# Out projection and the whole second MLP product as seven products; operand tiles moved by 32 bytes

## Chip, core and metric

One core of one Trainium2 chip runs the kernel in one launch. The metric is the device time of the launch in microseconds. TensorE does the matmuls, VectorE and ScalarE prepare their operands and read their results, GpSimd computes a few columns, SyncE and GpSimd issue DMAs.

## Reference

The kernel computes one layer of a streaming encoder on x of 512 frames by 1024 channels, all in float32:

```
h    = rmsnorm(x);  zu, zv, zq, zf, zi, zo, g_a, g_b = split(h @ w_in)
y_a  = gmlp_branch(zu, zv) @ w_up_a
y_b  = hgrn2_branch(zq, zf, zi, zo) @ w_up_b
mix  = sigmoid(g_a) * y_a + sigmoid(g_b) * y_b
x    = x + mix @ w_out                       # 1024 x 1024
h    = rmsnorm(x)
x    = x + square(relu(h @ w_ff1)) @ w_ff2   # 1024 x 4096, 4096 x 1024
out  = rmsnorm(x)
```

## The kernel before

**Products.** A float32 product is made of three matmuls of reduced-precision parts: `split` writes a high part H (ScalarE, a copy with rounding) and a low part L (VectorE, source minus H), and `mm3` multiplies H by H, H by L and L by H. `operand` splits a weight tile of 128 x 1024 into the rings `WH` and `WL` of five buffers each; `wload` loads it first by DMA on SyncE's queue into the ring `raw` of four buffers. So every weight tile costs one long ScalarE row and one long VectorE row.

**Seven products.** A product of 2 x 2 blocks can be made from seven products of sums of blocks in place of eight. Before the change this is so for the two merge gates and for ff1 (`seven`, 256-wide matmuls, partial sums on ScalarE and VectorE), and for channel tiles c=1, 2, 3 (of 1024 of the 4096 channels each) of the second MLP product, ff2. There the tile's activations `act` of 1024 channels by 512 frames fall into four quarters a[i,j] (i: half of the frames, j: half of the channels) and its weights into b11, b12, b21, b22. The weight sums w1 = b12 + b11 and w3 = b22 + b12 are made by a second DMA that adds to the tile (on GpSimd's queue, `accum_op`), the further sums w1 + b22 and w4 + w1 by VectorE, which also makes the sums of the activations (E, and in place) and the low parts `aL`, `WL`; ScalarE makes the high parts `aH`, `WH`. Each of the seven products is 24 matmuls, 512 wide, into two PSUM banks: X (tag `hm`), Z (`acc`), Y5 (`y`), Y3.

**Plain products.** The upb product (w_up_b), the out projection (w_out) and the first tile of ff2 (c=0, its eight tiles f < `NSLOW`) are plain. For the out projection the loop over channels d splits `mix` into mixH and mixL (192 matmuls, in two halves `hf` of the output columns and four frame tiles t); after each frame tile of the second half `norm_to_T` makes the norm: squares on ScalarE, the root on GpSimd, the scaled rows `xn` on VectorE, four transposes `pt` on TensorE, and the split of those into h2H and h2L. ff1 begins with four plain tiles (`NPLAIN`) in two halves of the frames; the first half needs h2 of frame tiles t=0 and 1.

**Order and memory.** A scheduler sets the order of the instructions on each engine when the program is built; on the chip each engine takes them in that order and waits at semaphores. The pool `po2` (E, aH, aL with three buffers, `rawx` for weights with six) lies where h2 and its sums lay, so nothing may be loaded there before ff1's last product has ended. The pool `pmix` holds mix.

Of the kernel before, what the change touches and what calls it, by code (L numbers as in the profile page):

```python
# [79 lines left out]


# [100 lines left out]


# [696 lines left out]
```

## Time and profile before

| what | us |
|---|---|
| time, median of 3 (lowest to highest) | 850.44 (847.4 to 851.98) |
| the profiled execution: its own time | 850.19 |
| its span in the profile | 848.4 |
| TensorE busy | 831.3 |
| VectorE busy | 637.3 |
| ScalarE busy | 401.4 |

The span is the time from the first to the last recorded instruction of that one execution; its own time is 1.8 us longer. Its mean granted TensorE clock is 0.995 of full speed. A matmul's recorded duration overlaps the next one's, so what a matmul costs is read from the distance of two starts.

### The profile page before, as it was taken

What the parts mean: (1) busy time and instruction counts of PE and PEld (TensorE: products, weight loads), DVE (VectorE), ACT (ScalarE), POOL (GpSimd) and SP (SyncE); (2) the same over time, 40 slices, a digit from 0 to 9 for tenths busy, and PEclk for the clock granted to TensorE, in tenths of its full rate; (3) what the DMA queues carried; (4) which work ended last, traced back from release to release, by engine and by line L of the source; (5) the groups of instructions that cost most, each with busy time, mean ns of one, the idle gap of its engine ahead of it and who ended that gap; (6) DMA issues with size and microseconds to landing.
All of it is one profiled execution on the core that took longest, in us unless ns stands there. A gap on an engine that the chain in (4) does not pass through costs nothing.

```text
span 848.4 us, 13369 instructions
## 1 busy us (share of the span) xinstructions
PE 831.3 (98%) x5282; PEld 748.2 (88%) x5282; DVE 637.3 (75%) x1092; ACT 401.4 (47%) x644; POOL 47.6 (6%) x79
## 2 busy tenths in 40 slices
PE   8999999999999999999999999899999999999996
PEld 6989898989889997999988889899999988777884
DVE  6563888979799587788565349877777574899996
ACT  6433434333342335556533333777766642545464
POOL 2000000000001000000000012000000000010103
PEclk9999999999999999999999999999999999999998
DMA  9233212121221122133423412222322285194812
GB/s 330 88 121 110 100 51 75 51 75 51 75 75 50 51 76 75 54 121 106 147 100 122 162 62 100 70 105 101 120 105 101 100 290 182 28 280 101 233 27 99
DMA packets 26912, 92.68 MB, mean 109 GB/s; under 512 B 3361, under 2 KB 3873, under 8 KB 26850
## 3 DMA queue, kind: packets, MB, share of 16 engines
q1 hardware_dynamic: 24546, 84.49, 28.1%
q0 software_dynamic: 1728, 6.29, 4.0%
q10 hardware_dynamic: 576, 1.05, 0.3%
q8 instruction: 41, 0.67, 0.3%
q14 instruction: 21, 0.17, 0.1%
HBM read 89.72 MB, written 2.10 MB: 108 GB/s over the span
## 4 chain that ended last, share of the span: by engine, by line
PE 88%; DMA 4%; DVE 3%; issue 2%; ACT 2%; POOL 0%; SPq 0%; POOLq 0%; ACTq 0%; DVEq 0%
PE acc L114 14%; PE acc L113 14%; PE acc L115 14%; PE prodx L115 5%; PE prodx L113 5%; PE prodx L114 5%; DMA raw<-in_w_dram 4%; PE prodzy L115 4%; PE prodzy L114 4%; PE prodzy L113 4%; PE sp L437 4%; PE hm L115 2%; PE hm L114 2%; PE hm L113 2%; PE y L113 2%
## 5 line engine op out<-in xcount | busy, mean ns | idle before, releaser
L90 DVE TENSOR_TENSOR WL<-raw,WH 128x1024 fp32r<-128x1024 f32 (+1 forms) x134 | 152.0, 1137 | 102.5 <-ACT WH L89 102.0
L89 ACT ACTIVATE WH<-raw 128x1024 fp32r<-128x1024 f32 (+1 forms) x134 | 132.4, 989 | 184.7 <-PE acc L114 68.4
L113 PE MATMUL acc<-WH,hTH 128*128 128x256 f32 x320 | 91.7, 287 | 0.5 <-ACT hTH L89 0.5
L115 PE MATMUL acc<-WH,hTL 128*128 128x256 f32 x320 | 91.6, 286 | 0.0
L114 PE MATMUL acc<-WL,hTH 128*128 128x256 f32 x320 | 90.6, 283 | 0.0
L115 PE MATMUL acc<-hTH,WL 128*128 128x512 f32 x160 | 64.3, 402 | 0.0
L114 PE MATMUL acc<-hTL,WH 128*128 128x512 f32 x160 | 64.1, 401 | 0.0
L113 PE MATMUL acc<-hTH,WH 128*128 128x512 f32 x160 | 64.1, 400 | 0.0
L90 DVE TENSOR_TENSOR WL<-s,WH 128x1024 fp32r<-128x1024 f32 x44 | 53.8, 1222 | 10.5 <-ACT WH L89 9.6
L113 PEld LDWEIGHTS acc<-WH,hTH 128*128 128x128 f32 x320 | 60.4, 189 | 0.7 <-ACT hTH L89 0.7
L115 PEld LDWEIGHTS acc<-WH,hTL 128*128 128x128 f32 x320 | 60.4, 189 | 0.1
L114 PEld LDWEIGHTS acc<-WL,hTH 128*128 128x128 f32 x320 | 60.3, 189 | 0.0
L89 ACT ACTIVATE WH<-s 128x1024 fp32r<-128x1024 f32 x44 | 46.7, 1061 | 14.1 <-PE prodx L114 8.7
L446 DVE COPY_PREDICATED scores<-mask,sp 128x192 f32<-128x192 int32 (+2 forms) x144 | 43.9, 358 | 6.8 <-PE sp L437 6.4
L114 PE MATMUL hm<-WL,aH 128*128 128x512 f32 x96 | 38.1, 397 | 0.0
L115 PE MATMUL hm<-WH,aL 128*128 128x512 f32 x96 | 38.0, 396 | 0.0
L113 PE MATMUL hm<-WH,aH 128*128 128x512 f32 x96 | 37.9, 396 | 0.0
L437 PE MATMUL sp<-QX,K 128*128 128x192 f32 x192 | 35.9, 326 | 0.0
L115 PEld LDWEIGHTS acc<-hTH,WL 128*128 128x128 f32 x160 | 30.1, 188 | 6.4
L114 PEld LDWEIGHTS acc<-hTL,WH 128*128 128x128 f32 x160 | 30.1, 188 | 6.4
L113 PEld LDWEIGHTS acc<-hTH,WH 128*128 128x128 f32 x160 | 30.1, 188 | 6.2
L89 ACT ACTIVATE WH<-rawx 128x1024 fp32r<-128x1024 f32 x24 | 25.1, 1052 | 19.3 <-issue 10.7
(298 smaller groups left out, 2417.1 us busy)
## 6 DMA issues: line engine op xcount, KB each, us to landing
raw<-in_w_dram SPq DMA_DIRECT2D x128, 512.0 KB, 3.5
rawx<-in_w_dram SPq DMA_DIRECT2D x18, 512.0 KB, 8.5
rawx<-in_w_dram POOLq DMA_DIRECT2D x6, 512.0 KB, 6.4
raw<-in_w_dram POOLq DMA_DIRECT2D x6, 512.0 KB, 9.0
x_t<-in_x_dram SPq DMA_DIRECT2D x4, 512.0 KB, 6.1
x<-in_x_dram SPq DMA_DIRECT2D x4, 512.0 KB, 5.7
out_dram<-x ACTq DMA_DIRECT2D x4, 256.0 KB, 2.8
out_dram<-x SPq DMA_DIRECT2D x4, 256.0 KB, 2.4
```

The costliest lines, as they stand in the source:

```text
L89: nc.scalar.activation(H, src, AF.Copy)
L90: nc.vector.tensor_tensor(L, src, H.bitcast(F32), ALU.subtract)
L113: nc.tensor.matmul(acc, ah, bh, start=first and i == 0, stop=False, **kw)
L114: nc.tensor.matmul(acc, ah, bl, start=False, stop=False, **kw)
L115: nc.tensor.matmul(acc, al, bh, start=False, stop=last and i == n - 1, **kw)
L437: nc.tensor.matmul(sp[:, j * 192:(j + 1) * 192].rearrange("p (g c) -> p g c", g=g), K[:, t * P:(t + 1) * P], QX[:, t * g:(t + 1) * g, 1:7, ...
L446: nc.vector.copy_predicated(scv[:, :, i0:i0 + n, :], mv[:, :, x0:x0 + n, :], spv[:, :, x0:x0 + n, :])
```

## The change

A class `Eighth` holds the seven products of one tile. It is used for the out projection (operand: quarters of mix, no longer split in the loop over d; `aH`, `aL` with two buffers; sums w1, w3 in `rawx` of `pmix`) and for all four channel tiles of ff2. 24 matmuls fewer are issued in each of the two places, 1624 of width 512 in place of 1672. For the out projection and for c=0 the products come as p1 (a11 b11), p2 (a12 w4), p5 (E w1), and then p6, and so on; w1 of c=0 is in `rawx`, no longer in `raw`. The norm of frame tiles 2 and 3 moves into the first stage of ff1, that of 0 and 1 stands around p4. `shift(pool)` puts a tile of 32 bytes into four pools, so that what is placed behind it in the pool moves by 32 bytes.

```diff
+    def shift(pool):
+        pool.tile([P, 8], F32, name="shift")
...
+    class Eighth:
+        def __init__(self, a, kind, c, pool, near=("b11", "w1"), bufs=3):
+            self.a, self.pool, self.bufs = a, pool, bufs
+            def fresh(name, *parts):
+                ts = [wp.tile([P, 1024], F32, tag="raw", bufs=4, name=name) if name in near else
+                      pool.tile([P, 1024], F32, tag="rawx", bufs=6, name=name) for k in range(2)]
+                for k, t in enumerate(ts):
+                    nc.sync.dma_start(t, A["w"][index[(kind, c, *parts[0], k)]])
+                    if len(parts) > 1:
+                        nc.gpsimd.dma_start(t, A["w"][index[(kind, c, *parts[1], k)]], accum_op=ALU.add)
+                setattr(self, name, ts)
+            parts = {"b11": [(0, 0)], "w1": [(0, 1), (0, 0)], "b22": [(1, 1)], "w4": [(1, 0)],
+                     "w3": [(1, 1), (0, 1)]}
+            for name in (*near, *(n for n in parts if n not in near)):
+                fresh(name, *parts[name])
+        def add(self, x, y):
+            for k in range(2):
+                nc.vector.tensor_tensor(x[k], x[k], y[k], ALU.add)
+        def operands(self, src, ring=False):
+            if ring:
+                return tuple(p.rearrange("p (k t) -> p k t", k=4) for p in operand(src, True))
+            H = self.pool.tile([P, 4, 256], F32R, tag="aH", bufs=self.bufs, name="aH")
+            L = self.pool.tile([P, 4, 256], F32R, tag="aL", bufs=self.bufs, name="aL")
+            split(src, H, L)
+            return H, L
+        def product(self, acc, hl, w, first, last, between=None):
+            H, L = hl
+            W = [operand(w[k]) for k in range(2)]
+            for i in range(2):
+                mm3(acc[i], [((H[:, k, i * P:(i + 1) * P], L[:, k, i * P:(i + 1) * P]),
+                              blk(W[k // 2], k % 2, 512)) for k in range(4)], (first, last))
+                if between and not i:
+                    between()
+        def p1(self, X, ring=False):
+            self.product(X, self.operands(self.a[0, 0], ring), self.b11, True, False)
+        def p2(self, Z, first, last):
+            self.product(Z, self.operands(self.a[0, 1]), self.w4, first, last)
+        def p5(self, Y5, first, last):
+            a = self.a
+            e = self.pool.tile([P, 4, 256], F32, tag="E", bufs=1, name="E")
+            nc.vector.tensor_tensor(e, a[1, 1], a[1, 0], ALU.subtract)
+            self.product(Y5, self.operands(e), self.w1, first, last)
+            nc.vector.tensor_tensor(a[1, 0], a[0, 0], a[1, 0], ALU.subtract)
+            nc.vector.scalar_tensor_tensor(a[0, 0], e, -1.0, a[0, 0], ALU.mult, ALU.subtract)
+            self.add(self.w1, self.b22)
+        def p6(self, X):
+            self.product(X, self.operands(self.a[0, 0]), self.w1, False, False)
+        def p7(self, X):
+            self.product(X, self.operands(self.a[1, 0]), self.w3, False, False)
+        def p3(self, Y3, first, last):
+            a = self.a
+            nc.vector.scalar_tensor_tensor(a[0, 1], a[0, 1], -1.0, a[0, 0], ALU.mult, ALU.subtract)
+            self.product(Y3, self.operands(a[0, 1]), self.b22, first, last)
+        def p4(self, X, between=None):
+            self.add(self.w4, self.w1)
+            self.product(X, self.operands(self.a[1, 1]), self.w4, False, True, between)
...
+    shift(pya)
...
+    shift(pt)
...
-    mixH = pmix.tile([P, KD, S], F32R, name="mixH")
-    mixL = pmix.tile([P, KD, S], F32R, name="mixL")
+    mix = pmix.tile([P, KD, S], F32, name="mix")
+    quarters = {(i, j): mix[:, 4 * j:4 * j + 4, 256 * i:256 * i + 256] for i in range(2) for j in range(2)}
...
-        nc.vector.tensor_tensor(sb, part[0][:, d, :], sb, ALU.add)
-        split(sb, mixH[:, d, :], mixL[:, d, :])
+        nc.vector.tensor_tensor(mix[:, d, :], part[0][:, d, :], sb, ALU.add)
+    proj = Eighth(quarters, "w_out", 0, pmix, ("b11", "w4"), 2)
...
+    shift(pr3)
...
-    for hf in range(2):
-        W = [wload("out", hf, k) for k in range(4)]
-        cs = slice(hf * 512, (hf + 1) * 512)
-        for t in range(NT):
-            acc = ps.tile([P, S], F32, tag="acc", bufs=2, name="acc")
-            tt = slice(t * P, (t + 1) * P)
-            mm3(acc, [((mixH[:, k, tt], mixL[:, k, tt]), blk(W[k // 2], k % 2, 512)) for k in range(KD)])
-            nc.vector.tensor_tensor(x2[:, t, cs], x2[:, t, cs], acc, ALU.add)
+    def add_to(l, m, src):
+        for i in range(2):
+            c = x2[:, 2 * l + i, m * S:(m + 1) * S]
+            nc.vector.tensor_tensor(c, c, src[i], ALU.subtract if m else ALU.add)
+    def squares2(l, m):
+        for i in range(2):
+            t = 2 * l + i
             junk = pn.tile([P, S], F32, tag="junk", bufs=1, name="junk")
-            mean_square(junk, x2[:, t, cs], ssq2[:, t, hf:hf + 1])
-            if hf == 1:
-                norm_to_T(pn, x2[:, t, :], t, ssq2[:, t, :], [gbc2[:, :S], gbc2[:, S:]], h2H, h2L)
+            mean_square(junk, x2[:, t, m * S:(m + 1) * S], ssq2[:, t, m:m + 1])
+    def norm2(t):
+        norm_to_T(pn, x2[:, t, :], t, ssq2[:, t, :], [gbc2[:, :S], gbc2[:, S:]], h2H, h2L)
+    def pair(name):
+        b = ps_f.tile([P, 2, S], F32, tag="zy", bufs=2, name=name)
+        return b[:, 0, :], b[:, 1, :]
+    X = [ps.tile([P, S], F32, tag="acc", bufs=2, name=f"X{i}") for i in range(2)]
+    proj.p1(X)
+    add_to(0, 0, X)
+    Y = pair("Z")
+    proj.p2(Y, True, True)
+    add_to(0, 0, Y)
+    squares2(0, 0)
+    Y = pair("Y5")
+    proj.p5(Y, True, True)
+    shift(pmix)
+    add_to(0, 1, Y)
+    add_to(1, 1, Y)
+    proj.p6(X)
+    add_to(0, 1, X)
+    Y = pair("Y3")
+    proj.p3(Y, True, True)
+    add_to(0, 1, Y)
+    squares2(0, 1)
+    proj.p7(X)
+    add_to(1, 1, X)
+    squares2(1, 1)
+    norm2(0)
+    proj.p4(X, lambda: norm2(1))
+    add_to(1, 0, X)
+    squares2(1, 0)
...
+            if half == 0 and f in (1, 2):
+                norm2(f + 1)
+    pn_stack.close()
...
-    for f in range(NSLOW):
-        aT[f] = operand(act[f])
-        W2[f] = wload("ff2", f)
-        if f < NSLOW - 2:
-            for t in range(NT):
-                for hf in range(2):
-                    ff2(f, t, hf)
-    for t in range(NT):
-        for hf in range(2):
-            for f in range(NSLOW - 2, NSLOW):
-                ff2(f, t, hf)
-            c = x2[:, t, hf * S:(hf + 1) * S]
-            nc.vector.tensor_tensor(c, c, eight[2 * t + hf], ALU.add)
...
+    for c in range(NF // 8):
+        one, end = c == 0, c == NF // 8 - 1
         a = {(i, j): acts[c][:, 4 * j:4 * j + 4, 256 * i:256 * i + 256] for i in range(2) for j in range(2)}
...
+        e = Eighth(a, "w_ff2", c, po2, ("b11", "w4") if one else ("b11", "w1"))
+        e.p1(X, one)
         add_to(0, 0, X)
+        if one:
+            e.p2(Z, True, False)
+        e.p5(Y5, one, end)
         if end:
             add_to(0, 1, Y5)
             add_to(1, 1, Y5)
+        e.p6(X)
         add_to(0, 1, X)
+        if not one:
+            e.p2(Z, False, end)
         if end:
             add_to(0, 0, Z)
             squares(0, 0)
             scaled(0, 0)
+        e.p7(X)
         add_to(1, 1, X)
         if end:
             squares(1, 1)
             scaled(1, 1)
+        e.p3(Y3, one, end)
         if end:
             add_to(0, 1, Y3)
             squares(0, 1)
             finish(0, 0)
+        e.p4(X)
```

What `shift` does to the addresses is read from the allocation of the two built programs. For each matmul, the addresses of the moving operand and of the weights are compared modulo 64 bytes: they are at equal places or 32 bytes apart. Matmuls by group:

| group (width) | before | after |
|---|---|---|
| in-projection on hT (512): 480 | apart | apart |
| upa on ya (512): 96 | apart | equal |
| 16 others of the gMLP branch (512) | equal | equal |
| upb on yb (512): 192 | equal | equal |
| out projection (512): 192, after 168 | apart | equal |
| ff2 c=0 (512): 192, after 168 | equal | equal |
| ff2 c=1 to 3 (512): 504 | apart | equal |
| on hT, and sums beside h2 and hT that lie apart (256): 1848 | apart | apart |
| t1, t2, t4 of the gates: 288, on h2: 864 (256) | equal | apart |

The first place where the order matters is VectorE at the end of the out projection and the start of ff1. Before, it reads (x_4794 is the residual rows, raw_5193 to raw_5205 weights of ff1):

```order
L619 TENSOR_TENSOR x_4794<-x_4794,acc 128x512
L228 SCALAR_TENSOR_TENSOR xn<-x_4794,rr_n,g_ffn 128x512 x2
L619 TENSOR_TENSOR x_4794<-x_4794,acc 128x512
L228 SCALAR_TENSOR_TENSOR xn<-x_4794,rr_n,g_ffn 128x512 x2
L90 TENSOR_TENSOR h2L<-pt,h2H 128x4x128 x2
L619 TENSOR_TENSOR x_4794<-x_4794,acc 128x512
L228 SCALAR_TENSOR_TENSOR xn<-x_4794,rr_n,g_ffn 128x512 x2
L90 TENSOR_TENSOR WL<-raw_5193,WH 128x1024
L90 TENSOR_TENSOR WL<-raw_5199,WH 128x1024
L90 TENSOR_TENSOR h2L<-pt,h2H 128x4x128 x2
L90 TENSOR_TENSOR WL<-raw_5205,WH 128x1024
L619 TENSOR_TENSOR x_4794<-x_4794,acc 128x512
```

After, the rows at that place are these (X_4823 and X_4824 are the two banks of X; raw_5475 and raw_5477 are the first weights of ff1's seven products, s their sums; the xn of t=0 and 1 are ahead of them):

```order
L702 TENSOR_TENSOR x_4803<-x_4803,X_4824 128x512
L92 TENSOR_TENSOR WL<-raw_5189,WH 128x1024
L702 TENSOR_TENSOR x_4803<-x_4803,X_4823 128x512
L92 TENSOR_TENSOR h2L<-pt,h2H 128x4x128 x2
L143 TENSOR_TENSOR s_5479<-raw_5477 128x512
L150 TENSOR_TENSOR s_5480<-raw_5475,raw_5477 128x512
L92 TENSOR_TENSOR WL<-raw_5195,WH 128x1024
L702 TENSOR_TENSOR x_4803<-x_4803,X_4824 128x512
L144 TENSOR_TENSOR s_5479<-s_5479,raw_5475 128x512
L92 TENSOR_TENSOR WL<-raw_5475,WH 128x1024
L310 SCALAR_TENSOR_TENSOR xn<-x_4803,rr_n,g_ffn 128x512 x2
L92 TENSOR_TENSOR h2L<-pt,h2H 128x4x128 x2
```

The first pair of h2L is that of frame tile 0 and the last pair that of frame tile 1; the read of the last X (X_4824 for the second time, the end of p4), a sum, a weight split and xn of frame tile 2 stand ahead of it. Before, the last read of the out projection (the last row of L619) stands behind the h2L of tile 1. From the row of L674 that reads the last upb product to the first of the last pair, the stretch has 29 rows of 1024 elements, 24 of 512 and 6 xn.

The second place is VectorE in ff2's first tile, c=0, of the changed program (act_5173 is the tile's activations, act_5174 those of c=1, w_7221 and w_7222 the two halves of w4, w_7225 and w_7226 those of w1, b_7231 the first of b22, hm the banks of X):

```order
L92 TENSOR_TENSOR WL<-w_7222,WH 128x1024
L246 TENSOR_TENSOR act_5173<-act_5173 128x4x256
L92 TENSOR_TENSOR aL<-act_5173,aH 128x1024
L247 SCALAR_TENSOR_TENSOR act_5173<-E,act_5173 128x4x256
L92 TENSOR_TENSOR aL<-E,aH 128x1024
L702 TENSOR_TENSOR x_4803<-x_4803,hm_7209 128x512
L258 SCALAR_TENSOR_TENSOR act_5173<-act_5173 128x4x256
L92 TENSOR_TENSOR aL<-act_5173,aH 128x1024
L244 TENSOR_TENSOR E<-act_5174 128x1024
L92 TENSOR_TENSOR aL<-act_5173,aH 128x1024
L246 TENSOR_TENSOR act_5174<-act_5174 128x4x256
L92 TENSOR_TENSOR WL<-w_7225,WH 128x1024
```

On ScalarE the same place reads:

```order
L91 ACTIVATE WH<-w_7222 128x1024
L162 ACTIVATE act_5176<-prodx 128x256
L91 ACTIVATE aH<-act_5173 128x1024
L772 ACTIVATE act_5176<-act_5176 128x1024
L91 ACTIVATE aH<-E 128x1024
L91 ACTIVATE aH<-act_5173 128x1024 x2
L91 ACTIVATE WH<-w_7225 128x1024
L91 ACTIVATE WH<-w_7226 128x1024
```

The low and high parts of all four operands and the start of c=1's E stand ahead of w1's split on VectorE; on ScalarE the operand of p7 stands ahead of it. Before, the eight plain tiles had one `WL` of activations and one of weights each there.

## Rows read from the trace of the kernel before

**Rows 1.** The page: busy us (share of span) and instructions of the engines.

```profile
PE 831.3 (98%) x5282; PEld 748.2 (88%) x5282; DVE 637.3 (75%) x1092; ACT 401.4 (47%) x644; POOL 47.6 (6%) x79
```

**Rows 2.** Windows in ff2: busy us (count) of PE, PEld, DVE, ACT, POOL; clock; DMA.

```profile
733.00:773.00 40.00, 39.10 (x165) 30.82 (x166) 38.63 (x39) 21.09 (x22) 3.49 (x4) 1.00 0.66 184
773.00:812.00 39.00, 39.00 (x169) 31.41 (x168) 36.94 (x38) 21.51 (x22) 3.50 (x4) 1.00 0.59 162
```

**Rows 3.** Timeline of PE: start, duration, line, form; upb and out projection.

```profile
457.55 0.39 PE L113 MATMUL acc<-ybH,WH 128*128 128x512 f32 x1
...
463.00 0.39 PE L113 MATMUL acc<-WH,mixH 128*128 128x512 f32 x1
...
468.59 0.40 PE L113 MATMUL acc<-WH,mixH 128*128 128x512 f32 x1
```

**Rows 4.** Timeline of PE: the 256-wide matmuls of the in-projection and ff1.

```profile
28.32 0.28 PE L113 MATMUL acc<-WH,hTH 128*128 128x256 f32 x1
...
31.88 0.28 PE L113 MATMUL acc<-WH,hTH 128*128 128x256 f32 x1
...
513.72 0.28 PE L113 MATMUL acc<-h2H,WH 128*128 128x256 f32 x1
...
520.91 0.28 PE L113 MATMUL acc<-h2H,WH 128*128 128x256 f32 x1
```

**Rows 5.** Timeline of VectorE: rows back to back, and the last upb read.

```profile
463.20 0.69 DVE L590 TENSOR_TENSOR part<-acc,part 128x512 f32<-128x512 f32 x1 [2.29 <-PE acc L115]
...
505.82 1.41 DVE L228 SCALAR_TENSOR_TENSOR xn<-x,rr_n,g_ffn 128x512 f32<-128x512 f32 x2 [1.88 <-POOL rr_n L209]
507.16 2.35 DVE L90 TENSOR_TENSOR WL<-raw,WH 128x1024 fp32r<-128x1024 f32 x2
509.43 1.28 DVE L90 TENSOR_TENSOR h2L<-pt,h2H 128x512 fp32r<-128x512 f32 x2
510.63 1.22 DVE L90 TENSOR_TENSOR WL<-raw,WH 128x1024 fp32r<-128x1024 f32 x1
```

**Rows 6.** The page: a group of splits on ScalarE; busy us, mean ns.

```profile
L89 ACT ACTIVATE WH<-rawx 128x1024 fp32r<-128x1024 f32 x24 | 25.1, 1052 | 19.3 <-issue 10.7
```

**Rows 7.** Timeline of PE: start of ff1.

```profile
510.17 0.66 PE L232 MATMUL pt<-ident,xn 128*128 128x128 f32 x4 [0.26 <-DVE h2L L90]
510.58 0.37 PE L114 MATMUL acc<-h2L,WH 128*128 128x256 f32 x1
```

**Rows 8.** Timeline of PE: first matmul of ff2, and the last of all.

```profile
676.07 0.40 PE L113 MATMUL hm<-WH 128*128 128x512 f32 x1
...
840.30 0.40 PE L115 MATMUL hm<-WH,aL 128*128 128x512 f32 x1
```

**Rows 9.** The page: DMA issues, KB each, median us to landing.

```profile
rawx<-in_w_dram SPq DMA_DIRECT2D x18, 512.0 KB, 8.5
rawx<-in_w_dram POOLq DMA_DIRECT2D x6, 512.0 KB, 6.4
raw<-in_w_dram POOLq DMA_DIRECT2D x6, 512.0 KB, 9.0
```

**Rows 10.** Timeline of PE: start of the gates' seven products.

```profile
335.29 0.38 PE L113 MATMUL prodx<-hTH,WH 128*128 128x256 f32 x1 [0.96 <-ACT WH L89]
...
336.56 0.39 PE L115 MATMUL prodx<-hTH,WL 128*128 128x256 f32 x1 [0.76 <-DVE WL L90]
...
337.72 0.38 PE L115 MATMUL prodx<-hTH,WL 128*128 128x256 f32 x1
...
341.14 0.30 PE L113 MATMUL prodx<-t2H,WH 128*128 128x256 f32 x1
```

**Rows 11.** Windows there and after the end of PE's work; clock as above.

```profile
338.00:339.00 1.00, 1.00 (x6) 1.00 (x6) 1.00 (x2) 1.00 (x3) 0.00 (x0) 0.50 0.93 369
844.00:846.00 2.00, 0.00 (x0) 0.00 (x0) 0.64 (x1) 0.61 (x1) 0.00 (x0) 0.50 0.80 299
```

More of the change, by code (lines that the diff above doesn't have):

```diff
@@ L29 @@
 NF = DFF // P
-NSLOW = 8
 RADIX = [1, 4, 16]
@@ L61, in _plan @@
     names += [("upb", d) for d in range(8)]
-    for hf in range(2):
-        names += [("out", hf, k) for k in range(4)]
+    names += [("w_out", 0, j, l, k) for j, l in QUARTERS for k in range(2)]
     names += [("ff1", f) for f in range(NF)]
-    names += [("ff2", f) for f in range(NSLOW)]
-    for c in range(NSLOW // 8, NF // 8):
-        names += [("ff2q", c, j, l, k) for j, l in QUARTERS for k in range(2)]
+    for c in range(NF // 8):
+        names += [("w_ff2", c, j, l, k) for j, l in QUARTERS for k in range(2)]
     return names
@@ L90, in split, with operand @@
         nc.vector.tensor_tensor(L, src, H.bitcast(F32), ALU.subtract)
-    def operand(src):
-        n = src.shape[-1]
+    def operand(src, quarter=False):
+        n = 1024 if quarter else src.shape[-1]
         H = wp.tile([P, 1024], F32R, tag="WH", bufs=NOPER, name="WH")
         L = wp.tile([P, 1024], F32R, tag="WL", bufs=NOPER, name="WL")
-        split(src, H[:, :n], L[:, :n])
+        if quarter:
+            split(src, *(p.rearrange("p (k t) -> p k t", k=4) for p in (H, L)))
+        else:
+            split(src, H[:, :n], L[:, :n])
         return H, L
@@ L689, in trunk_kernel @@
     X, Z, Y5, Y3 = banks(ps, "hm"), banks(ps, "acc"), banks(ps2, "y5"), banks(ps2, "y3")
-    ms = po2.tile([P, NT, 2], F32, name="ms")
-    def add_to(l, m, src):
-        for i in range(2):
-            c = x2[:, 2 * l + i, m * S:(m + 1) * S]
-            nc.vector.tensor_tensor(c, c, src[i], ALU.subtract if m else ALU.add)
+    ms = po2.tile([P, NT, 4], F32, name="ms")
     def squares(l, m):
@@ L719, in finish @@
             nc.scalar.dma_start(out[t * P:(t + 1) * P, m * S:(m + 1) * S], early)
[L721 to L757 removed]
+    for c in range(NF // 8):
+        one, end = c == 0, c == NF // 8 - 1
+        a = {(i, j): acts[c][:, 4 * j:4 * j + 4, 256 * i:256 * i + 256] for i in range(2) for j in range(2)}
+        e = Eighth(a, "w_ff2", c, po2, ("b11", "w4") if one else ("b11", "w1"))
+        e.p1(X, one)
         add_to(0, 0, X)
[L759 to L761 removed]
+        if one:
+            e.p2(Z, True, False)
+        e.p5(Y5, one, end)
         if end:
@@ L764, in trunk_kernel @@
             add_to(1, 1, Y5)
-        nc.vector.tensor_tensor(a[1, 0], a[0, 0], a[1, 0], ALU.subtract)
-        nc.vector.scalar_tensor_tensor(a[0, 0], e, -1.0, a[0, 0], ALU.mult, ALU.subtract)
-        add(w1, b22)
-        product(X, a[0, 0], w1, False, False)
+        e.p6(X)
         add_to(0, 1, X)
-        product(Z, a[0, 1], w4, one, end)
+        if not one:
+            e.p2(Z, False, end)
         if end:
@@ L774, in trunk_kernel @@
             scaled(0, 0)
-        add(w4, w1)
-        product(X, a[1, 0], w3, False, False)
+        e.p7(X)
         add_to(1, 1, X)
@@ L780, in trunk_kernel @@
             scaled(1, 1)
-        nc.vector.scalar_tensor_tensor(a[0, 1], a[0, 1], -1.0, a[0, 0], ALU.mult, ALU.subtract)
-        product(Y3, a[0, 1], b22, one, end)
+        e.p3(Y3, one, end)
         if end:
@@ L786, in trunk_kernel @@
             finish(0, 0)
-        product(X, a[1, 1], w4, False, True)
+        e.p4(X)
         add_to(1, 0, X)
@@ L819, in _weight_tiles @@
             t = chan(i["w_up_b"][0], name[1] * P, KD)
[L820 to L821 removed]
         elif kind == "ff1":
             t = chan(i["w_ff1"][0], name[1] * P, KD)
[L824 removed]
+        else:
             _, c, j, l, k = name
[L826 to L828 removed]
+            t = tok(i[kind][0], (8 * c + 4 * j + 2 * k) * P, 2, l * 512, 512)
         tiles.append(t)
```

45 lines of the change are left out of this document (removed).

## Prediction, made before the result was seen

> **What bounds the kernel now.** First the page's busy shares: TensorE is busy for 98% of the span and VectorE for 75% [rows 1], so a matmul less is worth its own time wherever nothing else becomes late. Then the windows of the second MLP product, which already runs as seven products for its channel tiles 1 to 3: in each stretch of 39 to 40 us VectorE is busy for 37 to 38.6 us beside TensorE's 39 [rows 2]. There the two engines are level, and that is the form of work that the change spreads. The reader is to see this first: seven products cost TensorE an eighth less, and VectorE far more (sums of weight and operand tiles, and splits of the sums).
>
> **Prices.** Starts in the timelines of the engines.
> - A 512-wide matmul: 24 of the upb product take 463.00 - 457.55 = 5.45 us, 227 ns each; the 24 of the out projection behind them take 5.59, 233 ns each [rows 3]. By the addresses (table in the section on the change) the operands of the first lie at equal places modulo 64 bytes, those of the second 32 bytes apart.
> - A 256-wide matmul: 60 of ff1's first stage in 7.19 us, 119.8 ns (equal places); 30 of the in-projection in 3.56, 118.7 ns (32 apart) [rows 4]. So the sign is the other way round, and the change moves each width to its better side. That the address is the cause is my reading; these rows also differ in their tiles.
> - VectorE, back to back: two 1024-wide rows 2.27 us, 1.135 each; two 512-wide 1.20, 0.60 each; two xn 1.34, 0.67 each [rows 5].
> - A split on ScalarE, 1024 wide: 1.05 us [rows 6].
>
> **A rule against the shift.** The Trainium skill, "TensorE: Matmul & The Clock Gate", Part 2, "Step-by-step: what each phase is for", says that TensorE reads its moving operand and its weights through two independent SBUF ports. By that the 32 bytes would change nothing; the 227 and 233 ns of [rows 3] do not bear it out as far as they go, and it stands below as a rival.
>
> **Out projection.** It loses 24 matmuls and the other 168 get the better place: 192 x 0.233 = 44.7 us become 168 x 0.227 = 38.1, which by TensorE alone is -6.6. But what has to be ready for ff1 comes from VectorE. Count from the end of the last upb product (463.20, where VectorE starts to read it [rows 5]). In the order of the changed program, from that row to the h2L of t=1, on which the third matmul of ff1 waits, VectorE has 29 rows 1024 wide, 24 of 512 and 6 of xn: 29 x 1.135 + 24 x 0.60 + 6 x 0.67 = 51.3 us without any idle time. TensorE has already met waits by then, the longest at p3: the split of its operand is the 19th long row, with ten short ones ahead, 27.6 us, where TensorE is at about 24.5. It would reach the matmul on h2L at about 46. Before, it was there at 510.58 - 463.20 = 47.4, with one group of four transposes more behind it (0.4) [rows 7]. So the stage ends 51.3 + 0.4 - 47.4 = **+4.3** later in place of 6.6 earlier. The order itself shows why: the read of the last X and xn of t=2 stand ahead of the h2L of t=1. Even if VectorE had kept up, after the last product of p4 there come 2 x 0.60 + 1.135 + 1.34 + 0.60 = 4.3 us of VectorE rows, so that the h2L could not come before 38.1 + 0.8 (the eight transposes of t=0) + 4.3 = 43.2: 43.2 + 0.4 - 47.4 = -3.8 is the other bound, and I take the sum of the rows, which has no idle time in it.
>
> **Second product, c=0.** 24 matmuls go. Count from the first matmul on it at 676.07 [rows 8]; twelve 256-wide matmuls of ff1 follow it in both programs (1.4 us). By TensorE alone the tile is 168 x 0.227 + 1.4 = 39.5 us. The weight w1 = (0,1)+(0,0) of this tile is new and lies where h2 lay, so its load starts when ff1 has ended, about 0.8 us in (behind g_fin); with 8.5 us for a load and 6.4 for the sum by DMA it lands at 15.7, or with the longer 9.0 at 18.3 [rows 9], and that would move the next number by 2 us at most. VectorE starts on E when the twelve narrow matmuls are done, 12 x 0.227 + 1.4 = 4.1, and from there to the split of w1's first half, it included, has 12 long rows and a short one: 4.1 + 12 x 1.135 + 0.60 = 18.3. By ScalarE alone: it splits a10 into a buffer that Z's operand has until 48 x 0.227 + 1.4 = 12.3, which takes until 13.4 [rows 6], and w1 only behind it; VectorE then has three long rows, 16.8, and no earlier w1 could change that. TensorE gets to the third matmul of Y5, which needs this split, at 50 x 0.227 + 1.4 = 12.8. Wait: 5.5. Next late is b22: its split stands eleven long rows behind, 18.3 + 12.5 = 30.8, where TensorE is at 18.3 + 48 x 0.227 = 29.2. Wait: 1.6. So c=0 ends at 39.5 + 5.5 + 1.6 = 46.6.
>
> **Second product, c=1 to 3.** The form is the old one with 227 for 233 ns: 3 x 38.1 = 114.4. VectorE's 29 long and 8 short rows of such a tile take 37.7, so there is hardly slack; I leave about the idle time that one window shows, 1.0 for the three (40.0 - 39.1 [rows 2]). The tail stays: 848.4 - 840.30 = 8.1 from the start of the last matmul [rows 8]. Together 46.6 + 114.4 + 1.0 + 7.9 (the last 0.2 of the tail's matmul is counted already) = 169.9, where before has 848.4 - 676.07 = 172.3: **-2.4**.
>
> **The rest.** The 96 matmuls on ya gain 6 ns each, 0.6; the 1152 narrow ones that move gain 1.1 ns, 1.3: **-1.9**. Norm of t=2, 3 inside ff1's first stage, the longer `ms` and the moved splits of mix lie beside matmuls: VectorE is already past more of its rows there than before, since the wait has let it catch up.
>
> **The clock.** Two waits of 1 us, ended at 335.29 and 336.56, were followed by a granted clock of 0.50 (the 1.2 GHz level), the next 16 matmuls taking 341.14 - 337.72 = 3.4 us, 214 ns each in place of 119: 1.5 us lost. At the end, idle from 840.7, it is at 0.50 in 844 to 846, as it was in 338 to 339 [rows 10, 11]. The changed program has three new waits of 3.1, about 5 and 5.5 us. I take the loss of one such fall, **+1.5** (bounds: none, and three times 3.4/2 = 1.7).
>
> **Sum.** +4.3 - 2.4 - 1.9 + 1.5 = +1.5 on the profiled execution's 850.19, which lies 0.25 below the median: **about 852**.
>
> **Rivals.**
> - *VectorE does not hold it up* (shorter rows on other addresses, or fewer waits than counted; the 37 us of 39 that it managed with TensorE at full pace speak for it, the row sum against): -3.8 in the out stage, c=0 with the least wait of 4.0 (16.8 - 12.8), 43.5 and so -5.5 in ff2, -1.9, no clock loss: 839; with no wait at all it would be 850.2 - 6.6 - 10.5 - 1.9 = 831. Faster, 0.20.
> - *The clock falls at every new wait* (p3, start of ff1, Y5): 3 x 1.7 = 5.1 for 1.5: 855.3. It decides from the third fall on. Slower, 0.12. The fall at 338 speaks for it; that there one fall answers to two waits speaks against.
> - *VectorE bounds c=1 to 3 as well*: each takes the 40.0 of the window at 733 again, not 38.5: +4.5, 856.2. It decides once VectorE's rows take over 39.5 us per tile in place of 37.7. Slower, 0.09.
> - *The 32 bytes do nothing*: c=1 to 3 get 1.0 longer each (less the 1.0 of waits that go), c=0 0.5, the rest 1.9: +4.4, 856. Slower, 0.09. By the rule of the Trainium skill it would be this one.
>
> **How the numbers follow.** My forecast has 0.47 and by itself 848 to 856; 0.03 stays for what I have not thought of. Half a per cent, what a measurement of this kernel tells from no change, is 846.2 to 854.7. Faster: the first rival and a little, 0.21. Same: 0.39 of the forecast and 0.04 of the others, 0.43. Slower: the rest, 0.36. The range reaches into the first rival, 843, and over the last three, 859.
>
> **What would show it.** Right: a wait of 4 to 6 us of the matmul acc on h2L for VectorE at the start of ff1, with no idle VectorE ahead of it; one of 4 to 6 us at the first Y5 for w1's split; 227 ns spacings in ya, the out stage and ff2, and 38.2 us per tile in c=1 to 3. Wrong: out stage under 47 us, no wait at Y5, spacings of 233, or a clock of 0.50 in long stretches.

## The result and the profile after

The changed kernel takes 863.43 us (median of 4 runs, 862.53 to 865.13) where the kernel before takes 849.02 (4 runs, 847.4 to 851.98): a ratio of 1.0167, interval 1.0139 to 1.0195. It is slower by 14.4 us, outside the range that was given. The execution profiled here took 863.53, its span is 861.8.

The page's busy line of the changed kernel, which answers to [rows 1]:

```profile
PE 827.1 (96%) x5234; PEld 742.6 (86%) x5234; DVE 679.4 (79%) x1126; ACT 417.7 (48%) x654; POOL 56.7 (7%) x87
```

TensorE does 48 matmuls fewer and is busy for 4.2 us less in a span that is 13.4 us longer: 17.6 us of new idle time. And 48 matmuls less should have taken 11 us from its busy time (48 x 0.23), not 4.2: some of those that remain run slower. The list of TensorE's waits from the end of upb on (us in total, times, longest) says for whom:

```profile
PE y L118 <- ACT WH L91: 8.2, 2, 4.2
PE acc L119 <- DVE h2L L92: 4.2, 1, 4.2
PE Y L120 <- DVE aL L92: 3.4, 2, 2.9
PE hm L118 <- ACT act L162: 1.3, 1, 1.3
```

And the timeline of TensorE says where (start, duration, line, form, idle time ahead of it; the pairs of rows without a wait serve to read a spacing, below):

```profile
464.04 0.39 PE L118 MATMUL X<-WH,aH 128*128 128x512 f32 x1
...
471.52 0.39 PE L118 MATMUL Z<-WH,aH 128*128 128x512 f32 x1
...
489.35 0.50 PE L120 MATMUL Y<-WH,aL 128*128 128x512 f32 x1 [2.90 <-DVE aL L92]
...
515.55 0.58 PE L119 MATMUL acc<-h2L,WH 128*128 128x256 f32 x1 [4.16 <-DVE h2L L92]
...
679.32 0.40 PE L118 MATMUL hm<-WH 128*128 128x512 f32 x1
...
684.97 0.50 PE L118 MATMUL hm<-WH 128*128 128x512 f32 x1 [1.30 <-ACT act L162]
...
697.56 0.73 PE L118 MATMUL y<-WH,aH 128*128 128x512 f32 x2 [3.97 <-ACT WH L91]
...
727.78 0.40 PE L120 MATMUL hm<-WH,aL 128*128 128x512 f32 x1
732.37 0.75 PE L118 MATMUL y<-WH,aH 128*128 128x512 f32 x2 [4.19 <-ACT WH L91]
...
769.64 0.39 PE L118 MATMUL hm<-WH,aH 128*128 128x512 f32 x1
...
774.54 0.40 PE L118 MATMUL hm<-WH,aH 128*128 128x512 f32 x1
...
775.24 0.63 PE L118 MATMUL y<-WH,aH 128*128 128x512 f32 x2
...
814.44 0.63 PE L118 MATMUL y<-WH,aH 128*128 128x512 f32 x2
```

With the first read of the last upb product (461.52, first row of the next block) these give the stages, each against the same two rows of before ([rows 5], [rows 7], [rows 8]):

| stretch | before | after | difference | forecast |
|---|---|---|---|---|
| start to the last upb read | 463.2 | 461.5 | -1.7 | -0.9, without the clock |
| to the first matmul on h2L | 47.4 | 54.0 | +6.6 | +3.9 |
| to the first matmul of ff2 | 165.5 | 163.8 | -1.7 | -0.6, without the clock |
| to the end of the span | 172.3 | 182.5 | +10.2 | -2.4 |

(The +4.3 of the out stage was made of this +3.9 and 0.4 for transposes that move behind the mark, here in the third row.) The forecast's sign was right in three stretches, but in the first and the third that is partly luck. In the first, the first matmul on ya starts 1.4 us later in this execution (309.99 for 308.56), and the clock's fall of before at 338 does not occur. In the third, the clock costs 2.5 us (below), and a wait that before has in ff1 is not there any more (list of TensorE's waits of before):

```profile
PE prodx L113 <- ACT WH L89: 1.6, 1, 1.6
```

Most of the miss is in ff2.

**Out stage.** The timeline of VectorE, the changed kernel:

```profile
461.52 0.69 DVE L674 TENSOR_TENSOR part<-acc,part 128x512 f32<-128x512 f32 x1 [2.89 <-PE acc L120]
...
496.02 1.23 DVE L92 TENSOR_TENSOR WL<-w,WH 128x1024 fp32r<-128x1024 f32 x1 [2.12 <-ACT WH L91]
...
501.47 2.76 DVE L310 SCALAR_TENSOR_TENSOR xn<-x,rr_n,g_ffn 128x512 f32<-128x512 f32 x4 [0.17 <-POOL rr_n L291]
...
513.48 1.41 DVE L310 SCALAR_TENSOR_TENSOR xn<-x,rr_n,g_ffn 128x512 f32<-128x512 f32 x2
514.81 0.68 DVE L92 TENSOR_TENSOR h2L<-pt,h2H 128x512 fp32r<-128x512 f32 x1
```

And that of ScalarE, with two rows of ff2 for the next point:

```profile
494.92 1.06 ACT L91 ACTIVATE WH<-w 128x1024 fp32r<-128x1024 f32 x1 [7.90 <-PE Y L120]
...
696.45 1.06 ACT L91 ACTIVATE WH<-w 128x1024 fp32r<-128x1024 f32 x1 [1.94 <-DMA w<-in_w_dram]
...
731.26 1.06 ACT L91 ACTIVATE WH<-w 128x1024 fp32r<-128x1024 f32 x1 [7.82 <-DMA w<-in_w_dram]
```

From the last upb read at 461.52 to the h2L of t=1 at 514.81 VectorE takes 53.3 us. The prediction's 51.3 us of rows include that h2L row; the rows ahead of it are 50.7 of them. Idle time of 2.12 us at 496.02 and of 0.17 at 501.47 makes 2.3 us of the difference; the other 0.3 is rows a little longer than counted. The reader follows that wait across three engines: VectorE waits for ScalarE's high part, ScalarE has waited until 494.92 for TensorE to release a buffer of the ring with product Y, and TensorE is late there because of its own 2.90 us at 489.35, which was for VectorE, and of the half clock behind that (below). A wait on one engine came back to it through the ring of operands.

**ff2.** The two long waits, at 697.56 and 732.37, are both for ScalarE's split of w1, and both times the bracket of that split in the block above names the load. The wait in c=0 was forecast. The one in c=1 was not; the queues of c=1's w1 show why. SyncE's loads:

```profile
708.14 9.47 SPq L202 DMA_DIRECT2D w<-in_w_dram  x6
```

GpSimd's adding loads:

```profile
721.15 0.86 POOL L204 DMA_DIRECT2D w<-in_w_dram  x1 [2.22 <-DMA w<-in_w_dram]
726.52 0.86 POOL L204 DMA_DIRECT2D w<-in_w_dram  x1 [4.51 <-DMA w<-in_w_dram]
```

In c=0 it is w4 that lies in the ring `raw` beside b11, and p4, the last product, still reads it. w1 of c=1 wants that ring, so its load is among the last of the row that ends at 708.14 + 9.47 = 717.6, the second adding load is issued at 726.52, and ScalarE can split only at 731.26. Before, w1 stood in `raw` in each of the tiles in seven products (c=1 to 3) and its buffers came free in the middle of the tile. From the starts in the block of TensorE, c=0 took 48.7 us (679.32 to the end of its last product, 727.78 + 0.23), c=1 47.2 (to 775.24) and c=2 39.2 (to 814.44), where 46.6 and three times 38.1, with 1.0 of idle time for the three, were forecast.

**The clock.** Windows of the changed kernel (busy us and count of PE, PEld, DVE, ACT, POOL; granted clock; DMA):

```profile
488.00:492.00 4.00, 2.65 (x9) 2.15 (x10) 4.00 (x6) 0.00 (x0) 0.00 (x0) 0.83 0.00 0
492.00:496.00 4.00, 4.00 (x15) 3.17 (x14) 1.89 (x2) 1.06 (x1) 0.00 (x0) 0.75 0.25 77
...
516.00:520.00 4.00, 4.00 (x21) 4.00 (x21) 4.00 (x6) 0.60 (x1) 0.00 (x0) 0.50 0.38 131
...
700.00:704.00 4.00, 4.00 (x15) 3.17 (x14) 4.00 (x5) 1.06 (x1) 0.00 (x0) 0.72 0.64 126
...
736.00:740.00 4.00, 4.00 (x11) 3.10 (x10) 4.00 (x5) 1.61 (x2) 0.00 (x0) 0.53 0.00 0
740.00:780.00 40.00, 40.00 (x173) 32.25 (x172) 37.87 (x38) 21.54 (x21) 3.45 (x4) 1.00 0.62 178
```

Behind each of the four waits of 2.9 us and more the granted clock falls to or towards 0.50, the 1.2 GHz level. From the starts of the matmuls in these stretches, against their spacing at full clock, the falls cost 1.6 us in the out stage, 2.5 at the start of ff1 and 3.8 in ff2 (1.3 and 2.5). The fall of before at 338 [rows 11] does not occur in this execution. ff2's +10.2 is then, to 0.1: waits +10.5 (12.3 for 1.8, with the slower starts of the matmuls right behind them), clock +3.8, matmuls -4.4 (672 of 233.3 ns for 192 of 227 and 504 of 233.3), and 0.2 at the end.

### The profile page after: what moved, and what is told of

The parts are those of the page before. It is cut to its first block, busy times and chain, and to the rows that moved or that the text cites. A ratio compares the mean times of both kernels' runs of the same rounds, so it can differ in the third digit from the quotient of the medians.

```text
span 861.8 us, 13356 instructions
## 1 busy us (share of the span) xinstructions
PE 827.1 (96%) x5234; PEld 742.6 (86%) x5234; DVE 679.4 (79%) x1126; ACT 417.7 (48%) x654; POOL 56.7 (7%) x87
## 4 chain that ended last, share of the span: by engine, by line
PE 84%; DVE 7%; DMA 4%; ACT 2%; issue 2%; POOL 0%; SPq 0%; POOLq 0%; ACTq 0%; DVEq 0%
PE acc L119 13%; PE acc L120 13%; PE acc L118 12%; PE prodx L120 5%; PE prodx L118 5%; PE prodx L119 5%; DMA w<-in_w_dram 4%; PE sp L520 4%; PE prodzy L119 4%; PE prodzy L120 4%; PE prodzy L118 4%; DVE WL L92 3%; PE hm L118 3%; PE hm L119 3%; PE hm L120 3%
## 5 line engine op out<-in xcount | busy, mean ns | idle before, releaser
L92 DVE TENSOR_TENSOR WL<-raw,WH 128x1024 fp32r<-128x1024 f32 x100 | 110.9, 1109 | 74.1 <-ACT WH L91 73.5
L91 ACT ACTIVATE WH<-raw 128x1024 fp32r<-128x1024 f32 x100 | 96.4, 966 | 123.8 <-PE acc L119 50.4
L91 ACT ACTIVATE WH<-w 128x1024 fp32r<-128x1024 f32 x50 | 52.3, 1055 | 78.6 <-DVE w L216 13.8
L92 DVE TENSOR_TENSOR WL<-w,WH 128x1024 fp32r<-128x1024 f32 x50 | 60.8, 1224 | 12.6 <-ACT WH L91 12.6
L119 PE MATMUL hm<-WL,aH 128*128 128x512 f32 x120 | 47.7, 398 | 0.0
L120 PE MATMUL hm<-WH,aL 128*128 128x512 f32 x120 | 47.7, 397 | 0.0
L118 PE MATMUL hm<-WH,aH 128*128 128x512 f32 x120 | 47.6, 399 | 0.0
L204 POOL DMA_DIRECT2D w<-in_w_dram x20 | 17.6, 878 | 415.7 <-DMA w<-in_w_dram 254.3
```

The costliest lines, as they stand in the source:

```text
L91: nc.scalar.activation(H, src, AF.Copy)
L92: nc.vector.tensor_tensor(L, src, H.bitcast(F32), ALU.subtract)
L118: nc.tensor.matmul(acc, ah, bh, start=first and i == 0, stop=False, **kw)
L119: nc.tensor.matmul(acc, ah, bl, start=False, stop=False, **kw)
L120: nc.tensor.matmul(acc, al, bh, start=False, stop=last and i == n - 1, **kw)
L204: nc.gpsimd.dma_start(t, A["w"][index[(kind, c, *parts[1], k)]], accum_op=ALU.add)
```

## The experiments

Each is compared with runs of the kernel before on the same chip; a ratio has its 95% interval behind it. Diffs are against the changed kernel where nothing else is said.

### Where the time went: one part back at a time

**Out projection plain again**, ff2 as changed (the loop over `hf` and t of before):

```diff
-    proj = Eighth(quarters, "w_out", 0, pmix, ("b11", "w4"), 2)
...
+    for hf in range(2):
+        W = [wload("out", hf, k) for k in range(4)]
```

> The changed kernel with the plain out projection of before; all four tiles of ff2 in seven products and the shifts stay. Theory: the stage from upb to ff1 goes back to 47.4 us and no clock falls behind it, 8 to 10 us off, 854 to 856. Rival (the loss is all in ff2): 862 or more.

Measured: 856.91 us, ratio 1.0105 (1.0085 to 1.0124). The waits of TensorE from 460 us on keep the two on w1:

```profile
PE y L119 <- ACT WH L92: 7.3, 2, 3.8
```

**c=0 plain again**, out projection as changed:

```diff
+    for f in range(NSLOW):
+        aT[f] = operand(act[f])
+        W2[f] = wload("ff2", f)
...
-    for c in range(NF // 8):
+    for c in range(1, NF // 8):
```

> The changed kernel with tile c=0 of ff2 as eight plain tiles, as before; out projection in seven products and the shifts stay. Theory: ff2 is as before (170.9 us from ff1's end, measured so there), so the stage from the last upb product to ff1 and the clock behind it is what is left: 6.65 + about 2.5 of the clock, less 2 to 4 that the shifts give: 852 to 856. Rival (the out projection costs nothing, all of the loss is in ff2): 846 or less.

Measured: 852.69 us, 1.005 (1.0032 to 1.0068). Behind the start of ff1 no wait over 0.7 us is left, that of c=1 is gone as well: it was a consequence of what c=0 does.

**The shifts alone**, in the kernel before (diff against it):

```diff
+    shift(pya)
...
+    shift(pt)
...
+    shift(pr3)
...
-    ms = po2.tile([P, NT, 2], F32, name="ms")
+    ms = po2.tile([P, NT, 4], F32, name="ms")
```

> The kernel before with nothing but the moved addresses of the change (32 bytes in the pools of ya, of the gates' sums and of h2, and the longer ms). Theory (the address sets the spacing of the matmuls): the 1152 narrow ones on h2 and on the gates' sums go from 119.7 to about 116.8 ns (3.3 us), the 96 on ya from 233 to 228 (0.5 us), aH of ff2 stays at 233: 3 to 4 us faster than before. Rival (operand and weights have ports of their own, the address is nothing): no change, and the spacings of the changed kernel had another cause.

Measured: 845.17 us, 0.9943 (0.9928 to 0.9959), 4.2 us faster. The narrow matmuls on h2, in equal places before, are now 32 bytes apart; 15 of them (timeline of TensorE, first and sixteenth) take 1.75 us, 116.7 ns each, for 119.8 in [rows 4]:

```profile
516.51 0.28 PE L117 MATMUL acc<-h2H,WH 128*128 128x256 f32 x1
...
518.26 0.28 PE L117 MATMUL acc<-h2H,WH 128*128 128x256 f32 x1
```

The traces say the same by stages. The out stage takes 47.4 us with the plain out projection and 54.0 with the plain c=0; from the first matmul of ff2 to the end it is 181.7 and 172.3, where before has 47.4 and 172.3.

So the three parts by themselves: the shifts -4.2; the seven products of the out projection 4.7 + 4.2 = +8.9 (from c=0 plain, which has the shifts); those of c=0 8.9 + 4.2 = +13.1. Their sum, 17.8, is 3.4 more than the 14.4 measured. In the profiled executions both partial kernels show the clock's fall at 338 and the changed kernel does not; at some 1.5 us each that is of this size, but one profile of each doesn't settle it.

### The waits on w1 in ff2

**c=0 with b11 and w1 in `raw`** and the order of the other tiles:

```diff
-        e = Eighth(a, "w_ff2", c, po2, ("b11", "w4") if one else ("b11", "w1"))
+        e = Eighth(a, "w_ff2", c, po2, ("b11", "w1"))
...
-        if one:
-            e.p2(Z, True, False)
-        if not one:
-            e.p2(Z, False, end)
+        e.p2(Z, one, end)
```

> The changed kernel with tile c=0 of ff2 in the order and with the buffers of the other tiles (b11 and w1 in raw, w4 in rawx, products p1, p5, p6, p2, ...). Theory (the two waits of 5.2 and 5.4 us at Y5 of c=0 and c=1 come from where w1 and w4 lie: w1 of c=0 may only be loaded after ff1, and w4 of c=0 keeps two raw buffers until p4, which the w1 of c=1 needs; each wait also halves the clock, 1.9 and 3.2 us): both waits and both falls go, 10 to 15 us off, about 851. Rival (VectorE's work for seven products in c=0 is the cause, whatever the order): the waits move to p6 or p2 and at most 4 us come off, 859 or more.

Measured: 854.52 us, 1.0083 (1.0063 to 1.0103): 6.6 us above before on its chip, for the changed kernel's 14.4; by the traces ff2 takes 174.6 us for 182.5. That lies between the theory and the rival. The wait on w1's high part is 0.5 in all, but a new one has come, on the first operand. ScalarE's timeline:

```profile
685.42 1.06 ACT L91 ACTIVATE WH<-w 128x1024 fp32r<-128x1024 f32 x1 [5.65 <-DMA w<-in_w_dram]
686.38 0.37 ACT L162 ACTIVATE act<-prodx 128x256 f32<-128x256 f32 x1
```

TensorE's waits from 520 us on:

```profile
PE hm L118 <- ACT act L162: 4.7, 1, 4.7
```

A split of a weight that has not landed now stands on ScalarE ahead of the last of `act`, which everything in c=0 needs. Which instruction waits in an engine's queue has been exchanged, not removed.

**w4 in `raw` for all tiles**, the order as changed:

```diff
-        e = Eighth(a, "w_ff2", c, po2, ("b11", "w4") if one else ("b11", "w1"))
+        e = Eighth(a, "w_ff2", c, po2, ("b11", "w4"))
```

> The changed kernel with the buffers of c=0 for all four tiles of ff2: b11 and w4 in raw, w1 in rawx. Theory (w1 of c=1 comes late only because w4 of c=0 keeps two raw buffers until p4): the wait of 5.4 us at Y5 of c=1 and the half clock behind it, 3.2 us, go; the wait at Y5 of c=0 stays: 855 to 858. Rival (the DMA queues are full there and any buffer comes as late): 861 or more.

Measured: 855.28 us, 1.0063 (1.005 to 1.0076). One wait on w1's high part is left in the list of TensorE's waits, that of c=0:

```profile
PE y L118 <- ACT WH L91: 4.7, 1, 4.7
```

That tells the cause of c=1's wait: the ring that its w1 was to be loaded into, not VectorE's rows, of which there are as many here.

### The out stage: rows of VectorE or something else

**Without the four weight sums** of the out projection (`add` does nothing there, so w1 + b22 and w4 + w1 are left out):

```diff
         def add(self, x, y):
+            if self.bufs == 2:
+                return
```

> The changed kernel without the four sums of weight tiles in the out projection (w1 + b22 and w4 + w1 are left out, so the projection's values are other ones; all other work and the order stay). Theory (VectorE's rows set the end of the stage): 4 x 1.135 = 4.5 us less from the last upb product to the first matmul on h2L, 54.0 to about 49.5, with shorter waits at p3 and less half clock: 4 to 7 us off, 857 to 859. Rival (the rows behind the last X, or the weights' arrival, set it): 53 or more in the stage, 862 or more.

Measured: 857.71 us, 1.0103 (1.0084 to 1.0122). The timeline of TensorE at the first matmul on h2L:

```profile
509.43 0.58 PE L119 MATMUL acc<-h2L,WH 128*128 128x256 f32 x1 [4.24 <-DVE h2L L92]
```

The window in which the changed kernel's clock is 0.83:

```profile
488.00:492.00 4.00, 4.00 (x20) 3.30 (x19) 4.00 (x5) 3.41 (x4) 0.00 (x0) 1.00 0.24 65
```

From its last upb read (461.28) that is 48.15 us for 54.03. Four rows of 1.135 us, 4.5, bring 5.9, since with them the wait at p3 and its fall of the clock go, and VectorE's idle time in this stretch falls from 2.3 to 0.9. The last wait stays 4.2: TensorE also gets there earlier. VectorE's rows set the end of this stage.

**The same sums on GpSimd:**

```diff
-                nc.vector.tensor_tensor(x[k], x[k], y[k], ALU.add)
+                (nc.gpsimd if self.bufs == 2 else nc.vector).tensor_tensor(x[k], x[k], y[k], ALU.add)
```

> The changed kernel with the four weight sums of the out projection (w1 + b22, w4 + w1) on GpSimd in place of VectorE; all else in the same order. Theory (VectorE's rows up to the h2L of t=1 set the end of the stage): four long rows less, 4.5 us, bring the first matmul on h2L from 54.0 to 49 to 50 us behind the last upb product, and with a shorter wait 4 to 6 us come off: 857 to 860. Rival (GpSimd is the slower one for such a sum, and w4 comes late, or the order of the norm sets the end): the stage stays at 53 or more, 863 or above.

Measured: 865.04 us, 1.0184 (1.017 to 1.0197), no better; the out stage is 56.9 us for 54.0. The timeline of GpSimd, its first two sums:

```profile
462.56 3.31 POOL L216 TENSOR_TENSOR w<-w,b 128x1024 f32<-128x1024 f32 x1 [27.45 <-DVE WL L92]
465.95 3.25 POOL L216 TENSOR_TENSOR w<-w,w 128x1024 f32<-128x1024 f32 x1
```

That of VectorE beside them:

```profile
462.39 1.22 DVE L244 TENSOR_TENSOR E<-mix 128x1024 f32<-128x1024 f32 x1
463.53 3.42 DVE L92 TENSOR_TENSOR aL<-mix,aH 128x1024 fp32r<-128x1024 f32 x1
466.88 3.41 DVE L246 TENSOR_TENSOR mix<-mix 128x1024 f32<-128x1024 f32 x1
```

A row of VectorE that takes 1.22 us alone takes 3.42 beside a GpSimd row of 3.31. These two sums saved VectorE 1.1 us each and cost it 2.2 each. The Trainium skill, "SBUF — State Buffer", section "SBUF: two separate sides", says that VectorE and GpSimd contend for one shared pair of ports as an exclusive lock, a VectorE operation with two SBUF inputs among them; the rows above agree.

### The clock

**34 matmuls that nothing uses**, ahead of the matmul on h2L, in the wait at the start of ff1:

```diff
+    for _ in range(34):
+        nc.tensor.matmul(first[1][:, :256], W[0][0][:, :P], h2H[:, 0, :256], start=True, stop=True, skip_group_check=True)
```

> The changed kernel with 34 matmuls of 256 columns that nothing uses (4.0 us) in the wait of 4.9 us for h2L at the start of ff1. Theory (the wait itself costs its length and then the halved clock on top, 3 to 6 us of matmuls at 213 ns): the granted clock stays at 1.00 at the start of ff1 and about 2 us come off: 861 to 862. Rival (the clock falls for another reason, or costs nothing): 863 to 864, clock 0.50 as before.

Measured: 860.34 us, 1.0128 (1.0102 to 1.0154). That is 11.6 us above before on its chip, for the changed kernel's 14.4, but the two intervals overlap; the stages say it more sharply. The out stage takes the same 54.0 us, and from the matmul on h2L to ff2 it is 161.2 for 163.8, 2.6 less, near the 2.5 worked out above. The window behind the wait, for 0.50 and 21 matmuls above:

```profile
516.00:520.00 4.00, 4.00 (x37) 4.00 (x36) 4.00 (x6) 0.60 (x1) 0.00 (x0) 1.00 0.44 131
```

VectorE is as late as before, but the clock stays at 1.00: at this place the fall follows TensorE's idle time and can be kept off by work of no use.

### The places of the operands

**`ms` of 128 bytes** (32 before, 64 in the change), so that aH and aL of ff2 move by another 64:

```diff
-    ms = po2.tile([P, NT, 4], F32, name="ms")
+    ms = po2.tile([P, NT, 8], F32, name="ms")
```

> The changed kernel with one edit: the tile ms has 128 bytes in place of 64, so that aH and aL of ff2 lie at a multiple of 128 bytes from the weights' high and low parts (64 beside a multiple before). Theory (what counts is equal places modulo 128 bytes, not 64): the 512-wide matmuls of ff2 go from 233 to 227 ns; 648 x 6 ns = 3.9 us at most, 2 to 4 us off the time, the less the more VectorE binds c=2 and c=3. Rival 1 (the address is not the cause): spacings stay 233, no change. Rival 2 (VectorE is the bound in c=2 and 3): spacings of 227 with new waits between them, no change in time.

Measured: 863.18 us, 1.019 (1.0172 to 1.0208), no gain. The 18 matmuls from the first row to the last take 4.19 us, 232.8 ns each:

```profile
761.59 0.39 PE L118 MATMUL hm<-WH,aH 128*128 128x512 f32 x1
...
765.78 0.39 PE L118 MATMUL hm<-WH,aH 128*128 128x512 f32 x1
```

**`ms` of 256 bytes** in the kernel with the shifts alone (with a shift ahead of mixH too, which left its spacing at 233):

```diff
-    ms = po2.tile([P, NT, 4], F32, name="ms")
+    ms = po2.tile([P, NT, 16], F32, name="ms")
```

> As the kernel before with the moved addresses, but ms has 256 bytes, so that aH and aL lie at equal places modulo 256 bytes with the weights (ya, yb and the out projection's aH in the changed kernel do, and have 227 to 228 ns; at 64 and at 128 bytes apart aH had 233 and 232). Theory (equal places modulo 256 count at this width): 504 matmuls of ff2 go to 227 ns, 3.0 us more than the run with ms of 64 bytes, 6 to 7 us faster than before; a part of it is lost if VectorE then binds c=1 to 3. Rival (traffic of VectorE, ScalarE and DMA in ff2 slows them): 233 again.

Measured: 843.60 us, 0.9926 (0.9912 to 0.994), 1.6 us less than the shifts alone for the 3.0 expected, and the two intervals overlap: it is the spacing that shows the effect. Here 18 matmuls of the same kind take 4.08 us, 226.7 each:

```profile
767.12 0.39 PE L117 MATMUL hm<-WH,aH 128*128 128x512 f32 x1
...
771.20 0.39 PE L117 MATMUL hm<-WH,aH 128*128 128x512 f32 x1
```

**And mix in equal places** as well (that shift behind mixL, not ahead of mixH):

```diff
-    shift(pmix)
     mixH = pmix.tile([P, KD, S], F32R, name="mixH")
     mixL = pmix.tile([P, KD, S], F32R, name="mixL")
+    shift(pmix)
```

> The kernel before with all shifts, ms of 256 bytes, and the plain out projection's mixH and mixL at equal places modulo 256 bytes with the weights as well. Theory: 192 matmuls from 233 to 227 ns, 1.2 us off the run with ms of 256 bytes; 7 to 8 us faster than before in all, as far as no clock fall hides it. Rival: those matmuls stay at 233, nothing more.

Measured: 842.43 us, 0.9921 (0.9902 to 0.9939); the matmuls on mix now come every 227.0 ns.

Taken together, by the distance of the moving operand's address from the weights' modulo 256 in the built programs: distance 0 has 226.7 to 227 ns per 512-wide matmul (yb, aH of the out projection, aH of ff2 and mix here); 32 and 96 have 233 (mix and ff2 before); 64 has 233.3 (ff2 after; in the timeline above 21 matmuls from 769.64 to 774.54); 128 has 232.8.

**Both**: that kernel with c=0 as seven products, w1 loaded first and in `raw`, the order of the other tiles (diff against that kernel):

```diff
+    for c in range(NF // 8):
+        one, end = c == 0, c == NF // 8 - 1
...
+        e = Eighth(a, "w_ff2", c, po2, ("w1", "b11") if one else ("b11", "w1"))
...
+        e.p2(Z, one, end)
```

> The aligned kernel with c=0 of ff2 in seven products as well, in the order and with the buffers of the other tiles and w1 loaded ahead of b11; the out projection stays plain. Theory (the loss of c=0 in the change was one of buffers and loads, not of VectorE's work): 24 matmuls less, 5.4 us, and 1 to 3 us of waits while E may not be written before ff1 has ended: 2 to 5 us less than the aligned kernel, 838 to 841. Rival (seven products of c=0 have no cover for their VectorE work at the change from ff1): waits of 5 us or more and a fall of the clock, 844 or more.

Measured: 841.51 us, 0.9911 (0.9894 to 0.9928): faster than both kernels of the change, but not told apart from the one above, which it was expected to beat by 2 to 5 us. The window over c=0 shows what is left to gain:

```profile
700.00:740.00 40.00, 40.00 (x178) 33.13 (x177) 39.82 (x40) 21.28 (x21) 3.49 (x4) 1.00 0.68 194
```

VectorE is busy for 39.82 of 40.00 us there, more than in [rows 2], and of the 5.4 us that 24 matmuls are worth 4.2 went to waits (1.3, 1.7 and 1.2 us in this kernel's list of TensorE's waits).

## Why the prediction was wrong, point by point

- **Out stage, +3.9 at the mark: right in kind, 2.7 too small (+6.6).** The count of rows held to 0.3 us once the idle time is taken out; leaving out four rows moved the end by more than their length. The wait at p3 came where it was forecast (27.8 us from the mark for 27.6) and as long (2.90 for 3.1). The step that failed is "without any idle time": it took VectorE for the head of the stage, while the ring of operands led that wait of TensorE and the half clock behind it back to VectorE, 2.1 us; another 0.2 was for GpSimd's root of the norm. The last 0.1 is that the matmul starts 0.74 us behind the start of its h2L row, for a row of 0.60.
- **c=0, 46.6 us (48.7 measured): the wait at Y5 right in size, 5.3 (3.97 for the high part, 0.53 for the low part behind it, and the slow starts of the matmuls between) for 5.5.** The load came 17.1 us after the first matmul (696.45 - 679.32), in the range of 15.7 to 18.3, and the bracket there names it: ScalarE stood 1.94 for it, VectorE only 0.6. "No earlier w1 could change that" was not tested by itself. The 1.6 for b22 did not show. In its place came a wait of 1.3 for the last of `act`, at 684.97, which had no term; the clock's fall took 1.3, and matmuls that kept 233 ns took 1.1.
- **"The form is the old one" for c=1 to 3: the step that failed most.** Each tile's work is the old one, but the buffers that c=0 leaves it are not. c=1's wait, 5.5 counted as above, and the clock's fall behind it, 2.5, had no term at all: c=1 took 47.2 us in place of 38.1. With w4 in `raw` everywhere, or c=0 plain, c=1's wait is gone. (TensorE's idle time for the high parts of w1 is 8.2 us in all here and 7.3 to 11.2 in the other kernels with both waits, so its size in one profile is not exact.)
- **227 for 233 ns in ff2: wrong.** The places were compared modulo 64 bytes; the experiments show that equal modulo 256 is what counts at this width. aH lay 64 apart and kept 233, 648 x 6 ns = 3.9 us that did not come. In the out projection, where they are equal modulo 256, the spacing was the predicted one (33 matmuls from 464.04 to 471.52, 226.7 each).
- **The rest, -1.9: too small.** The shifts alone gave -4.2. The 864 narrow matmuls on h2 gain about 3.1 ns each, not 1.1, which is 2.7. From the first matmul on ya to the gates' first the traces have 20.96 us for 21.41, 0.45 less for the forecast 0.6; and the gates, where the clock's fall at 338 is in both profiles (before and plain out projection), 84.6 for 85.2. Together that is 3.7; the rest is inside the interval.
- **The clock, +1.5 for one fall: wrong.** Every wait of 2.9 us and more was followed by a fall, 7.9 us in all, or about 6 more than the 1.5 of before.
- **The rivals.** "The clock falls at every new wait" is the mechanism that occurred, with one wait more than it counted and a larger price (2.0 us a fall for 1.7). "VectorE doesn't hold it up" fell with the no-sums kernel. "VectorE bounds c=1 to 3" did not occur: in the window from 740 to 780 VectorE is busy for 37.87 of 40 us and TensorE for all of them, and c=2 takes 39.2 us for the 40.0 of this rival. "The 32 bytes do nothing" is refuted by the shifts alone. The rule of two independent ports in the Trainium skill, "TensorE: Matmul & The Clock Gate", Part 2, "Step-by-step: what each phase is for", does not foresee 226.7 and 233 ns for matmuls that differ in their tile's place; the measurement decides.

## What to carry to other kernels

Before a saved matmul is counted, ask which engine prepares its operands, and follow the rings: a tile that stays in a shared ring until the last product of one stage delays the first loads of the next, where nothing was edited. A wait of TensorE is priced with what follows it, here 1.3 to 2.5 us at the lower clock for each wait of 3 to 4 us. And look at where the operands lie before a scheme is rebuilt: the places alone gave 0.8%, and seven products in c=0 on top of them nothing that can be told apart from it.

## What the runs showed of the hardware that was not expected

- The spacing of matmuls depends on where the two operands lie. 512 wide: 226.7 ns at equal places modulo 256 bytes, 233 at distances of 32, 64, 96 and 128. 256 wide, on h2, it is the other way: 119.8 at equal places modulo 64, 116.7 at 32 apart; but those of the in-projection, 32 apart too, take 118.7 [rows 4], so the distance is not all of it. Why is not shown by any run.
- A sum on GpSimd stretches VectorE's row with two inputs beside it from 1.22 to 3.42 us.
- The clock's falls at 338 and around 540 occur in some kernels' profiles and not in those of others that are alike up to there, so 2 to 3 us of a difference between single profiles may be theirs.
